# Conditioning sums by transposes and ScalarE, a one-operation GpSimd layer norm and bias-started accumulators in a two-layer hybrid decoder

## The chip, the core and the metric

One NeuronCore of a Trainium2 chip runs the whole program. The metric is the device time of one execution in microseconds, launch to end; the profile's span, from the first instruction to the last, is a little shorter. The engines are named as in the profile: PE (TensorE matmuls) and PEld (its weight loads), DVE (VectorE), ACT (ScalarE), POOL (GpSimd), SP (SyncE, which issues most DMAs).

## What is computed

256 tokens of width 2048 pass through two layers, all in float32. Each layer has a token mixer (forgetting attention in layer 0, sliding-window attention in layer 1) and a gated feed-forward with a short convolution (width 5632). Each of the four sub-layers is modulated by a conditioning vector `c` and closed by a layer norm:

```python
c_act = silu(c)                                   # (1, 2048)
for i in range(2):
    mod = c_act @ ada_w[i] + ada_b[i]             # ada_w[i]: 2048 x 12288
    sh1, sc1, g1, sh2, sc2, g2 = split(mod, 6)
    h = x * (1 + sc1) + sh1
    y = fox_attention(h) if i == 0 else swa_attention(h)
    x = layer_norm(ALPHA * x + (1 + g1) * y, ln_mix_g[i], ln_mix_b[i])
    h = x * (1 + sc2) + sh2
    y = (silu(conv(h @ w_up)[:, :5632]) * conv(h @ w_up)[:, 5632:]) @ w_down
    x = layer_norm(ALPHA * x + (1 + g2) * y, ln_ffn_g[i], ln_ffn_b[i])
```

The twelve vectors of `mod` are called (layer, index) below, index 0 to 5 for sh1, sc1, g1, sh2, sc2, g2. (0, 0) and (0, 1) are made in the opening; the other ten run in the background behind the matmuls of the layers.

## The kernel before

**Weights.** `stream` loads weights as tiles of 256 x 512 (512 KB) on SP's queue into a ring of ten buffers. For each, ACT rounds the tile to `wh` (line 258, the high half), DVE subtracts to get `wl` (line 269, the low half), and PE forms three products per block: high by high, high by low, low by high. With the activations as moving operand (`w_mm`, tile names `ws`) one tile is 24 matmuls of 256 columns; with the weights as moving operand (`x_mm`, `xs`) 12 of 512 columns.

**Order of the work.** `then` and `stream` put closures in the list `work`; `settle` takes them out about two weight tiles behind the loads. Before it runs a closure, `rest` looks through the next ones and writes the `wl` subtractions of up to two coming tiles. `tick` runs after each weight tile and advances the background: `ada_tick` adds `ada["rate"]` to a debt and makes one step of a conditioning vector per whole unit. `pin` keeps an instruction at its place; the others may be moved by the scheduler, which then fixes the order on each engine.

**Conditioning vectors** (`ada_vector`). One vector is 32 steps; each loads 512 KB of `ada_w` (`wa`) and adds its product with `cact` to `acc`, [128, 2048], by one DVE operation (line 384). The 128 partial sums of each column must then be added over partitions. For shifts and scales (columns) PE does it with 16 single-column matmuls against `ones` (`sums`, line 404, which the profile counts as 32 instructions), and DVE adds the bias (`finish`, line 408). (0, 4) and (1, 4) are held: their `sums` run in `release` at the layer norm where they are needed. Gates (rows, index 2 and 5) start from `acc` filled with zeros by POOL (line 373) with the bias loaded into its first row (line 374), and end in four matmuls of `ones` by 512 columns of `acc` (line 394). There is one `acc`.

**Boundaries.** Between two sub-layers PE has nothing to do: `residual` (lines 559 to 566, DVE) multiplies by the gate, adds to `x`, and takes statistics in quarters of 512 columns for the token halves t = 0 and 1; POOL makes the reciprocal deviation `rs` from variance + EPS by a power (lines 568, 569), and for t = 0 the product -mean * rs (571, 572), which ACT needs as bias. `normalise` then works on t = 0 on ACT (line 582) and on t = 1 on DVE (line 584), PE transposes (line 461), and `mod_pair` makes the halves `hH` and `hL` (lines 471 to 476, 84, 85). `between` sets this off; there are three boundaries, called 0 (before the first feed-forward), 1 (before the sliding-window attention) and 2 (before the second feed-forward), and a last layer norm at the end.

## Time and profile before

| What | Value |
|---|---|
| Time, median of 3 runs | 2310.31 us (2304.98 to 2312.66) |
| The profiled execution: its own time / its span | 2308.74 us / 2307.0 us |
| Granted TensorE clock, mean over the span | 0.982 of full speed |
| PE, DVE, ACT, POOL busy | 97%, 78%, 49%, 2% of the span |
| Weight and conditioning tiles read | 728 weight tiles, 320 conditioning tiles of 512 KB |

Stages, by the profile's time: opening and forgetting attention to about 500 us, first feed-forward 510 to 1265, sliding-window attention 1273 to 1544, second feed-forward 1552 to 2290, last layer norm to the end. Times in rows of the profile are in us from the start of the span. A busy PE is not PE at its best: matmuls overlap, and at half clock they are as busy as at full clock, so the column PEclk and the distance from one start to the next are to be read with it.

### The profile page before, as it was taken

How to read it: one execution, taken by the hardware profiler on the slowest of the kernel's cores; microseconds unless marked ns; L12 is line 12 of the kernel's file. 1: busy time of each engine (PE TensorE's matmuls, PEld its weight loads, DVE VectorE, ACT ScalarE, POOL GpSimd, SP SyncE). 2: the span in 40 equal slices, each digit the busy share in tenths (PEclk: the TensorE clock that was granted, in tenths of full speed). 3: DMA queues.
4: the chain of work that ended last, by engine and by line, in shares of the span. 5: the costliest groups of instructions: out<-in, count | busy, mean ns of one | idle time of the engine just before them, and what ended most of it. 6: DMA issues, size and time to landing. Idle time of an engine off the chain costs nothing.

```text
span 2307.0 us, 38669 instructions
## 1 busy us (share of the span) xinstructions
PE 2239.2 (97%) x15061; PEld 2056.8 (89%) x15061; DVE 1803.3 (78%) x2609; ACT 1136.8 (49%) x1685; POOL 43.0 (2%) x79
## 2 busy tenths in 40 slices
PE   6999999999999999999999999999999999999997
PEld 5899988779999988999987778779999988999986
DVE  7788978879977878868889978799887655666656
ACT  1335654445555533445533578845555533455532
POOL 1001000010000000000000000010000000000000
PEclk9899999999999999999999999999999999999999
DMA  9998999968887889878889676678887566666663
GB/s 325 311 332 282 338 329 346 335 217 306 298 280 229 292 318 323 290 239 282 288 276 348 200 237 194 217 265 276 264 277 244 179 193 193 192 187 189 189 194 110
DMA packets 285562, 598.86 MB, mean 260 GB/s; under 512 B 20791, under 2 KB 53817, under 8 KB 285377
## 3 DMA queue, kind: packets, MB, share of 16 engines
q1 hardware_dynamic: 284768, 595.85, 78.3%
q8 instruction: 118, 1.93, 0.3%
q0 software_dynamic: 608, 0.53, 0.1%
q14 instruction: 68, 0.55, 0.1%
HBM read 594.21 MB, written 2.10 MB: 258 GB/s over the span
## 4 chain that ended last, share of the span: by engine, by line
PE 88%; DVE 6%; ACT 2%; issue 1%; DMA 1%; POOL 0%; SPq 0%; DVEq 0%; ACTq 0%; POOLq 0%
PE ws L75 50%; PE xs L75 33%; DVE wl L269 2%; PE sm L75 1%; DVE acc L384 1%; DVE oacc L516 1%; PE cps L75 1%; PE S L75 1%; PE o L75 1%; ACT wh L258 1%; DMA w<-in_fox_w_in_dram 1%; PE sm L461 1%; PE T L655 0%; ACT pr L643 0%; ACT pr L635 0%
## 5 line engine op out<-in xcount | busy, mean ns | idle before, releaser
L269 DVE TENSOR_TENSOR wl<-w,wh 128x1024 fp32r<-128x1024 f32 x728 | 888.4, 1222 | 393.8 <-ACT wh L258 370.0
L258 ACT CAST wh<-w 128x1024 fp32r<-128x1024 f32 x728 | 763.6, 1051 | 859.3 <-PE ws L75 329.9
L75 PE MATMUL ws<-hH,wh 128*128 128x256 f32 x3328 | 941.8, 283 | 6.0 <-ACT wh L258 6.0
L75 PE MATMUL ws<-hL,wh 128*128 128x256 f32 x3328 | 934.8, 281 | 0.0
L75 PE MATMUL ws<-hH,wl 128*128 128x256 f32 x3328 | 932.6, 281 | 2.2 <-DVE wl L269 2.0
L75 PEld LDWEIGHTS ws<-hH,wh 128*128 128x128 f32 x3328 | 632.3, 190 | 10.0 <-ACT wh L258 6.8
L75 PEld LDWEIGHTS ws<-hL,wh 128*128 128x128 f32 x3328 | 632.0, 190 | 2.4 <-issue 1.9
L75 PEld LDWEIGHTS ws<-hH,wl 128*128 128x128 f32 x3328 | 630.4, 190 | 3.5 <-DVE wl L269 3.5
L75 PE MATMUL xs<-wh,gT 128*128 128x512 f32 x1408 | 436.8, 391 | 0.0
L384 DVE SCALAR_TENSOR_TENSOR acc<-wa,cact,acc 128x1024 f32<-128x1024 f32 x308 | 391.0, 1277 | 0.0
L75 PEld LDWEIGHTS xs<-wh,gT 128*128 128x128 f32 x1408 | 265.9, 189 | 55.3
L75 PE MATMUL xs<-wl,gT 128*128 128x512 f32 x704 | 275.1, 391 | 0.0
L75 PEld LDWEIGHTS xs<-wl,gT 128*128 128x128 f32 x704 | 133.0, 189 | 27.5
L75 PE MATMUL xs<-wl,hH 128*128 128x512 f32 x352 | 142.5, 405 | 2.9 <-DVE wl L269 2.9
L75 PE MATMUL xs<-wh,hH 128*128 128x512 f32 x352 | 142.3, 410 | 1.2 <-ACT wh L258 0.9
L75 PE MATMUL xs<-wh,hL 128*128 128x512 f32 x352 | 141.8, 405 | 0.4 <-DVE hL L85 0.4
L75 PE MATMUL xs<-wh,oT 128*128 128x512 f32 x384 | 125.3, 397 | 0.4 <-ACT pT L657 0.3
L985 ACT ACTIVATE u<-ws,ccol 128x256 f32<-128x256 f32 x176 | 96.6, 562 | 57.2 <-PE ws L75 50.2
L986 DVE SCALAR_TENSOR_TENSOR u<-ws,ccol,u 128x255 f32<-128x255 f32 x176 | 82.4, 477 | 19.1 <-ACT u L985 19.1
L75 PEld LDWEIGHTS xs<-wh,oT 128*128 128x128 f32 x384 | 72.8, 190 | 15.7 <-ACT pT L657 0.7
L75 PEld LDWEIGHTS xs<-wl,hH 128*128 128x128 f32 x352 | 67.8, 193 | 19.1 <-DVE wl L269 4.2
L988 DVE SCALAR_TENSOR_TENSOR u<-ws,ccol,u 128x254 f32<-128x254 f32 x176 | 83.2, 477 | 2.0
(211 smaller groups left out, 1568.1 us busy)
## 6 DMA issues: line engine op xcount, KB each, us to landing
w<-in_ffn_w_up_dram SPq DMA_DIRECT2D x352, 512.0 KB, 4.6
wa<-in_ada_w_dram SPq DMA_DIRECT2D x320, 512.0 KB, 5.2
w<-in_ffn_w_down_dram SPq DMA_DIRECT2D x176, 512.0 KB, 5.0
w<-in_fox_w_in_dram SPq DMA_DIRECT2D x96, 512.0 KB, 6.1
wo<-in_ada_w_dram SPq DMA_DIRECT2D x64, 512.0 KB, 7.2
w<-in_swa_w_in_dram SPq DMA_DIRECT2D x40, 512.0 KB, 5.1
w<-in_fox_w_o_dram SPq DMA_DIRECT2D x32, 512.0 KB, 6.4
w<-in_swa_w_o_dram SPq DMA_DIRECT2D x32, 512.0 KB, 5.4
```

What stands on the lines that cost most here:

```text
L75: return nc.tensor.matmul(o, lhsT, rhs, start=start, stop=stop, **kw)
L258: pin(nc.scalar.copy(h, w), False)
L269: pin(nc.vector.tensor_tensor(l, w, f32(h), op=ALU.subtract), False)
L384: pin(nc.vector.scalar_tensor_tensor(ac, wo, cact[:, k:k + 1], ac, op0=ALU.mult, op1=ALU.add), True)
L461: nc.tensor.transpose(o[:, t * P:(t + 1) * P], x[:, t, (k + j) * P:(k + j + 1) * P], ident)
L516: nc.vector.scalar_tensor_tensor(acc[:, v, k % 2, :], w[:, k, :], cact[:, kc:kc + 1], acc[:, v, k % 2, :], op0=ALU.mult, op1=ALU.add)
L985: nc.scalar.activation(u, pf, AF.Identity, bias=cw(CW, f), scale=cw(2, f))
L986: nc.vector.scalar_tensor_tensor(u[:, 1:], pf[:, :S - 1], cw(1, f), u[:, 1:], op0=ALU.mult, op1=ALU.add)
L988: nc.vector.scalar_tensor_tensor(u[:, 2:], pf[:, :S - 2], cw(0, f), u[:, 2:], op0=ALU.mult, op1=ALU.add)
```

## The change

- Four column vectors, (0, 3), (1, 0), (1, 1) and (1, 3), no longer end in `sums`. PE transposes `acc` in 16 blocks of 128 x 128, four into one PSUM bank at a step of the background, and ACT adds each block along its row, with an accumulating activation in place, one step later. The held vectors keep `sums`.
- Gates start from `acc` with the bias broadcast to all 128 partitions by one DMA of 1 MB, instead of the fill and the 8 KB DMA, and two steps of the background pass before the first product. The products use `cactp` = 128 * cact and the closing matmul `onep` = 1/128, so the bias counts once.
- Of the layer norm's scalar work POOL keeps the power alone. DVE adds EPS, and for t = 0 makes -mean * rs, just ahead of the last quarter's statistics of t = 1.
- `rest` counts certain closures as two tiles (`lone`), so the `wl` subtractions of tiles behind a boundary are no longer written ahead of it; the first two behind each boundary keep their place in the program (`behind`).
- The rates of the background are raised in four places: feed-forward 0 from 0.52 to 0.64 and 0.76 to 0.78, the output projection of layer 1 from 0.72 to 0.85.

```diff
+    onep = cst.tile([P, P], F32, name="onep")
+    nc.gpsimd.memset(onep, 1.0 / P)
...
+    cactp = cst.tile([P, KC], F32, name="cactp")
+    nc.gpsimd.tensor_scalar_mul(cactp, cact, float(P))
...
-    def then(fn):
+    def then(fn, alone=False):
+        if alone:
+            lone.add(fn)
...
         for f in items:
+            if f in lone:
+                n = max(n, 2)
             if f in residuals:
...
             def residual_(w=w, h=h, l=l, go=go):
-                pin(nc.vector.tensor_tensor(l, w, f32(h), op=ALU.subtract), False)
+                pin(nc.vector.tensor_tensor(l, w, f32(h), op=ALU.subtract), behind[0] > 0)
+                behind[0] -= 1
...
         if row:
-            pin(nc.gpsimd.memset(acc, 0.0), True)
-            nc.gpsimd.dma_start(acc[0:1, :], a["ada_b"][l:l + 1, v * D:(v + 1) * D])
+            nc.gpsimd.dma_start(acc, a["ada_b"][l, v * D:(v + 1) * D].partition_broadcast(P))
+            yield
+            yield
...
-                mm(ps, ones, acc[:, j * 512:(j + 1) * 512], start=True, stop=True)
+                mm(ps, onep, acc[:, j * 512:(j + 1) * 512], start=True, stop=True)
...
         else:
-            sums()
-            yield
+            tot = sp.tile([P, KC], F32, tag="tot", bufs=1, name="tot")
+            for k in range(0, KC, 4):
+                tb = bank()
+                for j in range(4):
+                    nc.tensor.transpose(tb[:, j * P:(j + 1) * P], part((k + j) * P, P), ident)
+                yield
+                for j in range(4):
+                    o = tb[:, j * P:(j + 1) * P]
+                    nc.scalar.activation(o, o, AF.Identity, accum_out=tot[:, k + j:k + j + 1])
+            yield
+            ps.append(tot)
             finish()
...
             if last:
+                if t == 1 and d == D // 512 - 1:
+                    mu, rs, nm = moments[0]
+                    pin(nc.vector.scalar_tensor_tensor(nm, mu, -1.0, rs, op0=ALU.mult, op1=ALU.mult))
                 nc.vector.bn_stats(stats[:, t, d, :], xs)
...
-                    nc.gpsimd.tensor_scalar_add(rs[:, 0:1], mv[:, 1:2], EPS)
-                    nc.gpsimd.tensor_tensor(rs[:, 0:1], rs[:, 0:1], mhalf, op=ALU.pow)
-                    if t == 0:
-                        nc.gpsimd.tensor_tensor(rs[:, 1:2], rs[:, 0:1], mv[:, 0:1], op=ALU.mult)
-                        nc.gpsimd.tensor_scalar_mul(rs[:, 1:2], rs[:, 1:2], -1.0)
+                    nc.vector.tensor_scalar_add(mv[:, 1:2], mv[:, 1:2], EPS)
+                    nc.gpsimd.tensor_tensor(rs[:, 0:1], mv[:, 1:2], mhalf, op=ALU.pow)
...
-            then(lambda d=d: defer(residual(ps[d], d, gates[l, 2], True)))
-        then(lambda: (flush(), ada.update(gate_free=True)))
+            then(lambda d=d: defer(residual(ps[d], d, gates[l, 2], True)), d == D // WB - 1)
+        then(lambda: (flush(), ada.update(gate_free=True)), True)
...
         modulate(*merged(l, v, g, b, ll), normalise)
+        behind[0] = 2
```

The feed-forward's last residual and flush and the calls of `between` are marked `alone` in the same way.

**PE, vector (1, 1) in the first feed-forward.** Before, the partition sums stand in one piece between the matmuls of the up-projection (`sm` is a PSUM bank, x16 are sixteen calls):

```order
L75 MATMUL ws<-hL,wh 128x256
L75 MATMUL ws<-hH,wl 128x256
L75 MATMUL sm<-ones,acc 128x1 x16
L75 MATMUL ws<-hH,wh 128x256
L75 MATMUL ws<-hL,wh 128x256
```

Now the first of four groups, with the up-projection's matmuls around it:

```order
L75 MATMUL ws<-hH,wh 128x256
L75 MATMUL ws<-hL,wh 128x256
L75 MATMUL ws<-hH,wl 128x256
L433 MATMUL sm<-ident,acc 128x128 x4
L75 MATMUL ws<-hH,wh 128x256
```

The sixteen single-column matmuls of this vector have become four groups of four transposes.

**DVE, boundary 1.** From the last product of the background before the boundary to the first low halves behind it, before (`t`, `stats` and `mv` belong to the residual and its statistics, `wl` to the first tiles of the next stage):

```order
L384 SCALAR_TENSOR_TENSOR acc<-wa,cact,acc 128x1024
L559 TENSOR_TENSOR t<-xs,gate 128x512
L561 TENSOR_TENSOR x<-x,t 128x512
L563 BN_STATS stats<-x 128x6
L559 TENSOR_TENSOR t<-xs,gate 128x512
L566 BN_AGGR mv<-stats 128x2
L269 TENSOR_TENSOR wl<-w,wh 128x1024
L561 TENSOR_TENSOR x<-x,t 128x512
L269 TENSOR_TENSOR wl<-w,wh 128x1024
L563 BN_STATS stats<-x 128x6
L566 BN_AGGR mv<-stats 128x2
L584 TENSOR_SCALAR x<-x,mv,rs 128x512 x3
```

Now the same stretch, first up to the normalisation of t = 1:

```order
L395 SCALAR_TENSOR_TENSOR acc<-wa,cactp,acc 128x1024 x2
L580 TENSOR_TENSOR t<-xs,gate 128x512
L582 TENSOR_TENSOR x<-x,t 128x512
L587 BN_STATS stats<-x 128x6
L590 BN_AGGR mv<-stats 128x2
L592 TENSOR_SCALAR mv<-mv 128x1
L580 TENSOR_TENSOR t<-xs,gate 128x512
L582 TENSOR_TENSOR x<-x,t 128x512
L586 SCALAR_TENSOR_TENSOR rs<-mv,rs 128x1
L587 BN_STATS stats<-x 128x6
L590 BN_AGGR mv<-stats 128x2
L592 TENSOR_SCALAR mv<-mv 128x1
```

and then, directly behind it:

```order
L605 TENSOR_SCALAR x<-x,mv,rs 128x512 x4
L493 TENSOR_SCALAR t<-sm,G,B 128x256 x2
L494 TENSOR_TENSOR hL<-t,hH 128x256 x2
L493 TENSOR_SCALAR t<-sm,G,B 128x256 x2
L494 TENSOR_TENSOR hL<-t,hH 128x256 x2
L277 TENSOR_TENSOR wl<-w,wh 128x1024 x2
```

The two `wl` have moved from the middle of the statistics to behind the first four low halves `hL`, one more product stands ahead of the residual, and all four quarters of t = 1 are normalised in a row instead of three.

**POOL, boundary 0.** Before (`rs` is the reciprocal deviation, `acc` the accumulator of (0, 5)):

```order
L568 TENSOR_SCALAR rs<-mv 128x1
L569 TENSOR_TENSOR rs<-rs,mhalf 128x1
L571 TENSOR_TENSOR rs<-rs,mv 128x1
L572 TENSOR_SCALAR rs<-rs 128x1
L568 TENSOR_SCALAR rs<-mv 128x1
L569 TENSOR_TENSOR rs<-rs,mhalf 128x1
L373 MEMSET acc 128x2048
L374 DMA acc<-in_ada_b_dram 1x16x128
```

Now, with the loads that stand ahead (`rows` are columns of weights for later):

```order
L164 DMA rows<-in_ffn_conv_w_dram 88x128 x3
L165 DMA rows<-in_ffn_conv_b_dram 88x128
L593 TENSOR_TENSOR rs<-mv,mhalf 128x1
L383 DMA acc<-in_ada_b_dram 128x2048
L593 TENSOR_TENSOR rs<-mv,mhalf 128x1
```

The fill is gone, and the DMA into `acc`, which waits for the held sums of (0, 4) on PE, stands ahead of the power of t = 1.

21 lines of the change are left out of this document (11 added, 10 removed).

## The prediction, made before the change was run

> **What bounds the kernel now.** I read the page first, then the busy times and the granted clock by stage, then the chain that ended last, and then the timeline around the two places where PE stands still. The page's busy times and its chain:
>
> ```profile
> PE 2239.2 (97%) x15061; PEld 2056.8 (89%) x15061; DVE 1803.3 (78%) x2609; ACT 1136.8 (49%) x1685; POOL 43.0 (2%) x79
> PE 88%; DVE 6%; ACT 2%; issue 1%; DMA 1%; POOL 0%; SPq 0%; DVEq 0%; ACTq 0%; POOLq 0%
> ```
>
> PE bounds nearly the whole span; what takes work or slow clock from PE in a full stage counts in full, and what speeds up another engine counts only where PE waits. The windows show where that is (busy us of PE, PEld, DVE, ACT and POOL, then the granted clock, the DMA share and GB/s):
>
> ```profile
> 400.00:450.00 50.00, 48.06 (x235) 39.71 (x234) 43.68 (x61) 25.03 (x49) 0.00 (x0) 1.00 0.97 334
> 450.00:500.00 50.00, 45.44 (x188) 35.88 (x187) 39.50 (x42) 16.75 (x16) 0.00 (x0) 0.97 0.86 289
> 500.00:510.00 10.00, 7.19 (x47) 6.25 (x46) 8.99 (x17) 5.78 (x10) 6.53 (x8) 0.71 0.35 114
> 529.60:687.00 157.40, 157.40 (x1348) 157.04 (x1346) 141.59 (x184) 85.47 (x116) 0.00 (x0) 1.00 0.89 301
> 1260.00:1280.00 20.00, 14.66 (x60) 11.31 (x59) 16.40 (x27) 10.03 (x14) 3.61 (x6) 0.83 0.57 214
> ```
>
> The feed-forward (fourth row) has no gap on PE. PE waits at the boundaries (third and fifth row: 2.8 and 5.3 us, and the clock drops too), and somewhat in forgetting attention's output projection (the first two rows), where DMA and DVE are nearly full.
>
> **Part 1, the column sums in the first feed-forward.** The chain shows the sums of (0, 3), (1, 0), (1, 1) and (1, 3) as links of their own (start, us):
>
> ```profile
> 383.00 3.46 PE sm L75 x32
> 855.81 3.48 PE sm L75 x32
> 1013.25 3.88 PE sm L75 x32
> 1186.94 3.52 PE sm L75 x32
> ```
>
> The last three lie in the feed-forward: 3.48 + 3.88 + 3.52 = 10.9 us of PE. What follows them shows in the granted clock; the columns are PE busy, clock, DMA share, GB/s:
>
> ```profile
> 386.30:390.00 3.70, 3.70 (x18) 1.00 0.80 268
> 859.10:862.50 3.40, 3.40 (x10) 0.50 0.38 124
> 1016.10:1022.90 6.80, 6.80 (x34) 0.50 0.53 157
> 1190.20:1193.60 3.40, 3.40 (x10) 0.50 0.59 174
> ```
>
> PE is "busy" through all of them, but behind each of the three the clock stands at half, for 3.4, 6.8 and 3.4 us. Half of that is lost: 1.7 + 3.4 + 1.7 = 6.8 us, of which 0.4 is in the 3.88 already, so 6.4. Behind (0, 3) it stays at 1.00. The cost before is 10.9 + 6.4 = 17.3 us.
>
> The new work is 48 transposes. The nearest row is twelve in one piece at full clock, from this start to the next matmul's:
>
> ```profile
> 1331.45 1.47 PE L934 MATMUL qp<-ident,qq 128*128 128x128 f32 x12
> 1332.68 0.48 PE L75 MATMUL xs<-wh,hL 128*128 128x512 f32 x1
> ```
>
> 1.23 us for twelve is 0.103 each, 4.9 us for 48. PE time alone gives -6.0. Four transposes last 0.41 us, and PE works fully on both sides, so I expect no half clock behind them and count the 6.4 too. I take -12; the bounds are -6.0 (slow windows come anyway) and -12.4. For (0, 3) the same step saves 3.46 - 1.65 = 1.8 us at 383, but behind it, from 430 on, PE waits for DVE and DMA (first two rows of the windows): 0, with -1.8 as a bound.
>
> On ACT the price comes from the attention's exponentials, also 128 x 128 with an accumulator:
>
> ```profile
> L635 ACT ACTIVATE pr<-pr,nm 128x128 f32<-128x128 f32 x96 | 43.4, 453 | 22.4 <-DVE nm L631 22.3
> L635 ACT ACTIVATION_READ_ACCUMULATOR pr<-pr,nm 128x1 f32 x96 | 18.0, 188 | 0.0
> ```
>
> At most 0.64 us each, 64 times, is 41 us in bursts of 2.6. ACT is at 85.47 of 157.40 us in the feed-forward and makes the weight halves two tiles ahead, so one burst a step is covered: 0. If a PSUM bank comes free late, PE waits: up to +3.
>
> **Part 2, the boundaries.** Boundary 1 before, first DVE, then PE:
>
> ```profile
> 1262.42 1.28 DVE L384 SCALAR_TENSOR_TENSOR acc<-wa,cact,acc 128x1024 f32<-128x1024 f32 x1
> 1263.62 0.69 DVE L559 TENSOR_TENSOR t<-xs,gate 128x512 f32<-128x512 f32 x1
> 1266.44 1.16 DVE L269 TENSOR_TENSOR wl<-w,wh 128x1024 fp32r<-128x1024 f32 x1
> 1268.11 1.22 DVE L269 TENSOR_TENSOR wl<-w,wh 128x1024 fp32r<-128x1024 f32 x1
> 1269.25 0.69 DVE L563 BATCH_NORM_STATS2 stats<-x 128x6 f32<-128x512 f32 x1
> 1269.96 0.26 DVE L566 BATCH_NORM_AGGREGATE mv<-stats 128x2 f32<-128x24 f32 x1
> 1271.21 1.46 DVE L584 TENSOR_SCALAR x<-x,mv,rs 128x512 f32<-128x512 f32 x3 [0.98 <-POOL rs L569]
> 1273.15 1.00 DVE L472 TENSOR_SCALAR t<-sm,G,B 128x256 f32<-128x256 f32 x2 [0.48 <-ACT hH L471]
> 1276.31 0.54 DVE L476 TENSOR_SCALAR t<-sm,G,B 128x256 f32<-128x256 f32 x1
> ```
>
> ```profile
> 1270.61 2.33 PE L461 MATMUL sm<-ident,x 128*128 128x128 f32 x8 [5.01 <-ACT x L582]
> 1273.76 0.63 PE L75 MATMUL xs<-wl,hH 128*128 128x512 f32 x1
> 1276.07 0.39 PE L75 MATMUL xs<-wh,hH 128*128 128x512 f32 x1
> ```
>
> The two `wl` leave the statistics, but they are 1.2 us each and one more product of 1.2 (1262.42 to 1263.62) now comes ahead, so the residual begins at 1264.8. Each half's steps take 0.7 each (statistics to aggregate, 1269.25 to 1269.96): t, x, statistics, then aggregate and EPS in an estimated 0.5, 2.65 in all; twice that ends at 1270.1. The power on POOL, 0.58 (first row of the fence on boundary 0), puts the normalisation at 1270.7, only 0.5 earlier than 1271.21. The new product -mean * rs on DVE waits for POOL's power of t = 0, with the last statistics queued behind it; the power can start at 1267.5 and needs 0.58, the product comes at 1268.9, so it adds nothing. What is late next is `wl`: PE's second matmul of the new stage needs it. Before it had long been made, at 1269.3; now it stands behind four normalisations (to 1272.6), two pairs of steps from L472 to the next L476 (1273.15 to 1276.31, 3.16) and its own 1.2, so at 1277.0. PE starts its second matmul there, not at 1273.76. Before it lost some time on `hL` and was at its sixth, at 1276.07; now it gets there at 1278.4 at full clock, or 1279.8 at half. I take +3.5. Bounds: -0.5 (`wl` is not waited for), +5.4 (a further 3.4 us at half clock).
>
> Boundaries 0 and 2 have a stall of another kind; POOL, DVE and PE at boundary 0:
>
> ```profile
> 505.12 0.58 POOL L569 TENSOR_TENSOR rs<-rs,mhalf 128x1 f32<-128x1 f32 x1
> 505.64 1.80 POOL L373 MEMSET acc<- 128x2048 f32 x1
> 507.74 0.62 POOL L374 DMA_DIRECT2D acc<-in_ada_b_dram  x1 [0.29 <-POOL acc L373]
> ```
>
> ```profile
> 505.73 2.00 DVE L584 TENSOR_SCALAR x<-x,mv,rs 128x512 f32<-128x512 f32 x1 [0.69 <-POOL rs L569]
> ```
>
> ```profile
> 500.24 3.63 PE L75 MATMUL sm<-ones,acc 128*128 128x1 f32 x32
> 511.22 0.28 PE L75 MATMUL ws<-hH,wl 128*128 128x256 f32 x1
> ```
>
> The first normalisation takes 2.00 us while POOL fills `acc`; three take 1.46 at boundary 1. Without the fill this 1.5 us goes. The DMA into `acc` now stands ahead of the power of t = 1 and waits for the held sums (500.24 + 3.63 = 503.9); 0.62 for its issue and 0.58 for the power put the normalisation at 505.1, its end at 505.7 instead of 507.7. But again `wl` is next: 505.1 + 1.9 (1271.21 to 1273.15) + 3.16 + 1.2 = 511.4, against 511.22 for PE's first matmul with `wl` before. The 2 us are given back. PE stands between and may keep half clock longer, so I take +1 for each of the two; bounds -2 (`wl` is not waited for) and +2.
>
> **Part 3, the rest.** In the first half of feed-forward 0, 1344 matmuls of weight tiles at 24 are 56 tiles in 157.4 us, 2.81 each, with 141.59 / 56 = 2.53 of DVE. A rate 0.12 higher adds 0.12 x 1.28 = 0.15: 2.68 of 2.81. It fits, with little room: +0.5, bounds 0 and +4. For the broadcast of 1 MB the nearest rows are:
>
> ```profile
> ln<-in_ln_ffn_g_dram SPq DMA_DIRECT2D x4, 512.0 KB, 4.5
> acc<-in_ada_b_dram POOLq DMA_DIRECT2D x4, 8.0 KB, 2.5
> ```
>
> Half of its size lands in 4.5 us; two steps of the background, over 4 us at 2.81 a tile, pass before the first product. At 334 GB/s 1 MB costs 3.1 us of the queues, which matters only for (0, 2) at 178 us, when they are full: +0.5, bounds 0 and +3. In the opening POOL's `onep` and `cactp` stand ahead of fills that DVE needs, but DVE waits longer for its first weights:
>
> ```profile
> 9.68 0.35 DVE L514 TENSOR_SCALAR oacc<-wo,cact 128x256 f32<-128x256 f32 x1 [6.15 <-DMA wo<-in_ada_w_dram]
> ```
>
> Those 6.15 us cover two small operations: 0, and without that cover about 1. The last layer norm loses POOL steps and gains DVE steps of like size: 0, within 0.5.
>
> Sum: -12 + 3.5 + 2 + 0.5 + 0.5 = -5.5. The profiled execution took 2308.74 us (span 2307.0), so 2303.2 of its kind. The median is 1.6 above it: 2304.8.
>
> **The rivals.** *The boundaries keep their gain*: -12 - 0.5 - 4 + 1 = -15.5, 2294.8. The normalised x is earlier at all three; against it stands the order on DVE. Chance 0.20. *Half clock behind each restart*: PE, idle until `wl`, keeps 0.50 for one or two more stretches of 3.4 us at three places, 5 to 10 us more: 2310 to 2315, 2312 in the middle. For it: 6.8 us at half clock at 1016. Chance 0.17. *DVE becomes the bound* in feed-forward 0, if its unevenness eats the 5% left: 157 x 0.05 = 8 in place of the 0.5, 2312.3; against it, PE has no gap at 90%. Chance 0.05.
>
> *The transposes slow the clock too*, the case on the slower side: each of the twelve groups in the feed-forward is followed by 3.4 us at half clock, 1.7 lost, 20.4 in all: -5.5 + 20.4 = +15, 2325. It decides from about four such groups. Against it: the twelve transposes at 1331.45 run at full pace to the next matmul. Chance 0.06. The Trainium skill, "TensorE: Matmul & The Clock Gate", Part 4: PE-mode transpose, says that full clock does not engage for transposes, as they do not count as PE work. By that rule a longer run of them would cost what the single-column matmuls cost; no run here yet shows four among full matmuls in the feed-forward.
>
> **How the numbers follow.** The forecast has 0.52, with its own range of -10 to 0 (2300 to 2310). A difference of 0.3%, 6.9 us, is about what a measurement can tell. Of the forecast a little over a third lies beyond it, 0.20; with the first rival 0.40 faster. Slower are the transposes' case and part of the half clock's: 0.10. The rest, 0.50, is within 0.3%. The range runs from the first rival's 2294 to 2315, the end of the half-clock case.
>
> **What would show it.** Right: no half clock around 855, 1013 and 1187 us in the granted clock, groups of four transposes near 0.41 us apart from their neighbours; at boundaries the normalisation earlier by 0.5 and 2 us, and PE's first wait behind it ended by `wl`. Wrong: half clock behind the groups, PE waiting for a PSUM bank that ACT holds, or PE's first `wl` matmul earlier than before against its transposes.

## The result, and the profile after

The changed kernel takes 2284.04 us (median of 6 runs, 2281.01 to 2287.92), the kernel before 2311.21 in the same comparison (6 runs, 2304.47 to 2312.66): a ratio of 0.9891 (95% interval 0.9874 to 0.9908), 25 us less. The prediction was 2304.8 with a range of 2294 to 2315, so the time lies 10 us below the range. The profiled execution took 2283.99 us, its span is 2282.1, its mean granted clock 0.988 against 0.982 before.

The page's busy times after, then the windows that answer to those of before (PE, PEld, DVE, ACT, POOL busy, granted clock, DMA share, GB/s):

```profile
PE 2222.3 (97%) x14997; PEld 2043.3 (90%) x14997; DVE 1801.9 (79%) x2621; ACT 1156.2 (51%) x1813; POOL 25.4 (1%) x61
```

```profile
400.00:450.00 50.00, 50.00 (x246) 41.89 (x246) 46.04 (x65) 25.51 (x50) 0.00 (x0) 1.00 0.94 340
450.00:500.00 50.00, 44.47 (x199) 36.54 (x197) 41.57 (x57) 20.21 (x24) 1.74 (x3) 0.89 0.79 284
490.00:500.00 10.00, 8.81 (x52) 8.01 (x50) 7.08 (x20) 6.52 (x11) 1.74 (x3) 0.62 0.26 105
520.00:677.40 157.40, 157.21 (x1323) 154.87 (x1322) 142.76 (x185) 84.81 (x118) 0.00 (x0) 1.00 0.89 305
1240.00:1260.00 20.00, 16.39 (x76) 13.07 (x75) 17.61 (x32) 12.27 (x19) 1.11 (x2) 0.91 0.48 168
```

PE is still the bound at 97%, with 17 us less of work. The feed-forward (fourth row) is full at a granted clock of 1.00, and DVE, 142.76 instead of 141.59 us there, still fits. Boundary 1 (last row) has 3.6 us without PE instead of 5.3 and a clock of 0.91 instead of 0.83. Boundary 0 (third row) has gained nothing in clock: 0.62, where the prediction's row of before has 0.71.

**The sums.** PE at the first group of vector (1, 0), and the windows behind this group and the last of (1, 3):

```profile
814.29 0.39 PE L75 MATMUL xs<-wh,gT 128*128 128x512 f32 x1
814.52 0.60 PE L433 MATMUL sm<-ident,acc 128*128 128x128 f32 x4
814.88 0.48 PE L75 MATMUL xs<-wh,gT 128*128 128x512 f32 x1
```

```profile
814.90:818.30 3.40, 3.40 (x18) 2.81 (x16) 1.23 (x1) 2.63 (x10) 0.00 (x0) 1.00 0.59 175
...
1138.70:1142.10 3.40, 3.40 (x18) 2.81 (x17) 3.20 (x8) 3.06 (x12) 0.59 (x1) 1.00 0.78 263
```

Four transposes take 0.36 us from their start to the next matmul's (0.41 was forecast), and the clock behind them is 1.00. ScalarE's part is 64 times 262 + 194 ns, 0.46 us each instead of at most 0.64:

```profile
L437 ACT ACTIVATE sm<-sm x64: 251/262/272, 381.8 to 1141.1; 128x128 f32<-128x128 f32 x64
L437 ACT ACTIVATION_READ_ACCUMULATOR sm<-sm x64: 180/194/197, 382.0 to 1141.3; 128x1 f32 x64
```

**Boundary 1**, DVE and then PE:

```profile
1242.40 0.69 DVE L580 TENSOR_TENSOR t<-xs,gate 128x512 f32<-128x512 f32 x1 [0.74 <-PE xs L75]
...
1248.41 1.92 DVE L605 TENSOR_SCALAR x<-x,mv,rs 128x512 f32<-128x512 f32 x4 [0.66 <-POOL rs L593]
...
1253.39 2.36 DVE L277 TENSOR_TENSOR wl<-w,wh 128x1024 fp32r<-128x1024 f32 x2
```

```profile
1247.51 0.66 PE L482 MATMUL sm<-ident,x 128*128 128x128 f32 x4 [2.43 <-ACT x L603]
1249.02 0.66 PE L482 MATMUL sm<-ident,x 128*128 128x128 f32 x4 [0.85 <-DVE x L605]
1250.00 0.68 PE L75 MATMUL xs<-wh,hH 128*128 128x512 f32 x1 [0.33 <-ACT hH L492]
1250.48 0.63 PE L75 MATMUL xs<-wl,hH 128*128 128x512 f32 x1
```

From the last quarters of the residual to the normalisation of t = 1 it is 6.0 us (1242.40 to 1248.41) instead of 7.6 (1263.62 to 1271.21). And PE's second matmul, the first on a low half, runs at 1250.48, while the two `wl` behind the boundary are made from 1253.39 on. They are not the ones it needs. PE's first wait at this boundary is ended by ScalarE's normalisation of t = 0: 2.43 us instead of the 5.01 in the prediction's row at 1270.61.

**Boundary 0**, POOL:

```profile
490.06 0.57 POOL L593 TENSOR_TENSOR rs<-mv,mhalf 128x1 f32<-128x1 f32 x1 [284.35 <-DVE mv L592]
494.83 0.61 POOL L383 DMA_DIRECT2D acc<-in_ada_b_dram  x1 [4.19 <-PE sm L75]
495.45 0.57 POOL L593 TENSOR_TENSOR rs<-mv,mhalf 128x1 f32<-128x1 f32 x1
```

This came as forecast: the DMA waits for the held sums and the power of t = 1 stands behind it. The clock did not. The stretch at half clock around this boundary, before and then after:

```profile
504.20:510.90 6.70, 4.22 (x17) 3.42 (x18) 5.76 (x14) 4.98 (x9) 3.18 (x4) 0.50 0.26 83
```

```profile
492.40:502.60 10.20, 9.01 (x41) 8.21 (x41) 7.49 (x20) 5.20 (x10) 1.18 (x2) 0.50 0.26 104
```

It is three times 3.4 us long instead of twice, and the extra 3.4 us cost up to half of that, 1.7.

### The profile page after: what moved, and what is told of

The parts are those of the page before. It is cut to its first block, busy times and chain, and to the rows that moved or that the text cites. A ratio compares the mean times of both kernels' runs of the same rounds, so it can differ in the third digit from the quotient of the medians.

```text
span 2282.1 us, 38648 instructions
## 1 busy us (share of the span) xinstructions
PE 2222.3 (97%) x14997; PEld 2043.3 (90%) x14997; DVE 1801.9 (79%) x2621; ACT 1156.2 (51%) x1813; POOL 25.4 (1%) x61
## 5 line engine op out<-in xcount | busy, mean ns | idle before, releaser
L395 DVE SCALAR_TENSOR_TENSOR acc<-wa,cact,acc 128x1024 f32<-128x1024 f32 x180 | 228.7, 1279 | 0.0
L395 DVE SCALAR_TENSOR_TENSOR acc<-wa,cactp,acc 128x1024 f32<-128x1024 f32 x128 | 163.0, 1279 | 1.8 <-DMA acc<-in_ada_b_dram 1.8
```

Of the source, the lines that this page charges most:

```text
L395: pin(nc.vector.scalar_tensor_tensor(ac, wo, (cactp if row else cact)[:, k:k + 1], ac, op0=ALU.mult, op1=ALU.add), True)
```

## Where the time went, by stage

To compare stages, the table takes the start of the same weight matmul, counted from the program's first (numbers 1000, 2300, 2600, 7540, 8000, 8380, 8600 and 13,700), and subtracts its start in the profiled execution of before; each cell is what a stage adds, in us. Eight kernels of the experiments below are in it too; for the others the text gives single stages, worked out in the same way. "Sliding, 1" has boundary 1 and the first half of the sliding-window stage.

| Kernel | opening | layer 0 from 240 us, with output projection | boundary 0 | feed-forward 0 | sliding, 1 | sliding, 2 | boundary 2 | feed-forward 1 |
|---|---|---|---|---|---|---|---|---|
| changed | -4.9 | -5.3 | +0.9 | -11.1 | -6.0 | -0.2 | +0.1 | +2.1 |
| before + sums | -2.6 | -5.4 | +1.2 | -11.5 | -4.1 | +5.5 | +17.5 | +5.9 |
| before + sums + rates | -4.6 | -5.4 | +1.6 | -10.5 | -2.6 | +2.8 | +0.3 | +2.0 |
| before + rates | -2.8 | +3.1 | +0.9 | +2.5 | -3.1 | +2.9 | +0.3 | 0.0 |
| before + order | +0.3 | -0.1 | -0.7 | +3.3 | -2.5 | +0.1 | -0.9 | +0.2 |
| changed, old order | -2.7 | -5.1 | +1.2 | -10.4 | -3.6 | -0.2 | -1.3 | +0.1 |
| changed, no turns | +1.2 | -5.5 | +0.8 | -9.1 | -4.1 | +2.9 | +0.3 | +0.2 |
| changed, split sums | -5.0 | -2.4 | -0.7 | -5.7 | -6.4 | -0.2 | -1.4 | +0.1 |
| changed, bias on SP | -3.0 | -5.2 | -1.3 | -11.1 | -6.9 | -0.2 | -2.0 | 0.0 |

The opening's column can't be put down to the change. Windows of 30 to 130 us of before, of before + order and of before + sums + rates, in which every engine has the same instructions in the same order far beyond this stretch, and of the changed kernel:

```profile
30.00:130.00 100.00, 91.02 (x561) 84.82 (x561) 78.31 (x170) 30.77 (x37) 0.00 (x0) 0.85 1.01 330
```

```profile
30.00:130.00 100.00, 89.41 (x557) 83.35 (x557) 77.69 (x169) 30.76 (x37) 0.00 (x0) 0.86 0.99 327
```

```profile
30.00:130.00 100.00, 89.21 (x593) 83.07 (x594) 80.98 (x176) 32.48 (x40) 0.00 (x0) 0.91 1.03 341
```

```profile
30.00:130.00 100.00, 89.22 (x594) 82.85 (x594) 81.28 (x177) 32.80 (x40) 0.00 (x0) 0.91 1.03 343
```

The first three have clocks of 0.85, 0.86 and 0.91 with the same instructions, and lie 4.9 us apart by 130 us. The last kernel's -4.9 is no different: the variant further down with the low half of tile 0 behind the boundary has the changed kernel's opening, instruction for instruction, and +0.9 there. Differences in the opening are left out of what follows; so are those in the second feed-forward (2 us in two kernels, 5.9 in before + sums), whose cause is open. Half clock comes in stretches of 3.4 us, each worth 1.7 us, and their number differs too: at boundary 0 it is three in the changed kernel and in before + sums, and two in before and with the split sums, though before + sums has the boundary of before and the split sums that of the changed kernel. So a difference of up to 2 us in one cell can be the execution's own.

## The experiments

Ratios are to runs of the kernel before on the same chip, with a 95% interval; a small difference is read from the stage, since the total has an uncertainty of some 4 us. The stages are those of one profiled execution, which can lie off its kernel's median: 6.3 us below it for the split sums, 5.4 above for before + order, 4.8 above for before + sums.

**The sums alone**: the new branch of `ada_vector` put into before, with nothing else of the change.

```diff
-            sums()
-            yield
+            tot = sp.tile([P, KC], F32, tag="tot", bufs=1, name="tot")
...
+            ps.append(tot)
             finish()
```

> The kernel before with the new sums alone (four column vectors by transposes and ScalarE), everything else as before. If the sums are worth what the prediction gave them, the three groups in the first feed-forward go with their half-clock stretches: 11.5 us less there (3.3, 4.9 and 3.4 at 856, 1013 and 1187 us), opening and boundaries as before, 2311.2 -> about 2299.7. Rival, the sums also move the background: the added steps of (0, 3) shift (0, 4) into another place and the output projection of forgetting attention loses its waits too, about 5 us more, 2295. Rival, the half clock would have come anyway: only PE time, 6 us, 2305, with half-clock stretches of 3.4 us still in the feed-forward.

Measured: 2310.37 us, 1.0007 (0.9998 to 1.0016). The feed-forward gains its 11.5 us and the output projection 5.4, and all of it is gone by the end. DVE and PE of this kernel at boundary 2:

```profile
1531.07 10.78 DVE L384 SCALAR_TENSOR_TENSOR acc<-wa,cact,acc 128x1024 f32<-128x1024 f32 x9
```

```profile
1540.71 3.57 PE L75 MATMUL sm<-ones,acc 128*128 128x1 f32 x16 [13.45 <-DVE acc L384]
```

A vector now takes five turns for its sums instead of one. At the old rates (1, 4) is still nine products short when the last statistics of boundary 2 are done, and they are made there in a row, with PE idle for 13.45 us and the clock at 0.50 from 1529.3 to 1556.5. The expectation saw the two gains and not this price.

**Sums and rates**, both put into before.

```diff
-            then(lambda i=i: ada.update(rate=((1.4,1.4,1.8,1.8), (0.72,)*4)[l][i]))
+            then(lambda i=i: ada.update(rate=((1.4,1.4,1.8,1.8), (0.85,)*4)[l][i]))
...
-            then(lambda: ada.update(rate=(0.52, 0.4)[l]))
+            then(lambda: ada.update(rate=(0.64, 0.4)[l]))
...
-                ada["rate"] = (0.76, 0.4)[l]
+                ada["rate"] = (0.78, 0.4)[l]
```

> The kernel before with the new sums and the new rates, without the gates, the layer norm's operations and the order. Theory: with the sums alone, the gain of 18 us up to boundary 2 is given back there, because vector (1, 4), whose turns come later by the steps that the sums now take, is not ready and PE waits 13.5 us for its products; the rates are there for this. So here the 11.5 us of the feed-forward and about 5 of the output projection of forgetting attention stay: 2308 - 17 = about 2291. Rival, the rates cost as much as they give (DVE fuller in the feed-forward and in the output projection of layer 1): 2300 or more.

2292.26 us, 0.9932 (0.992 to 0.9945). Boundary 2 costs 0.3 instead of 17.5. The first theory holds.

**The rates alone.**

> The kernel before with the new rates alone. The prediction on record gave them 0.5 us of cost, 0 to 4. If they are of use only because the new sums take more steps, nothing is gained here: 2308 to 2312. Rival, they gain by themselves, as vectors come off the end of the sliding-window stage where DVE is full: 2300 to 2306.

2310.66 us, 1.0003 (0.9992 to 1.0015): worth nothing by themselves.

**The changed kernel with the old rates.**

> The changed kernel with the old rates. Theory: as with the sums alone, (1, 4) is not ready at boundary 2; the two steps that a gate now waits make it later still by a step or two of 1.2 us: 13 to 20 us of PE standing there, 2284 -> 2297 to 2305. Rival, the order or the layer norm frees enough steps: under 3 us, 2284 to 2287. A third, by the prediction on record where the higher rates cost 0.5 us: 2283.5.

2306.95 us, 1.000 (0.999 to 1.001): by the medians 23 us of the gain are gone, by the ratio all of it, more than expected; boundary 2 alone is 19.7 us worse than in the changed kernel.

**The changed kernel with the old sums.**

> The changed kernel with the old sums (16 single-column matmuls in one piece). If the sums are worth 11.5 us whatever stands around them, 2284.0 -> 2295.5, with half clock for 3.4 to 6.8 us behind each of (1, 0), (1, 1) and (1, 3) and nothing else moved. Rival, the parts help each other: the rates were raised for vectors that take more steps, so with the old sums vectors end earlier than needed and move other waits, a difference of 5 us or more from 11.5, to be seen in the output projection (430 to 470 us) or in the sliding-window stage.

2306.37 us, 0.9999 (0.9989 to 1.0009): 22 us by the medians and the whole gain by the ratio, not 11.5. The feed-forward loses 9.9, the output projection 7.7, the second half of the sliding-window stage 3.0. So the rival holds: the value of the sums is not that of one stage.

**Splitting or transposing?** The changed kernel with single-column matmuls, in four groups:

```diff
-                for j in range(4):
-                    nc.tensor.transpose(tb[:, j * P:(j + 1) * P], part((k + j) * P, P), ident)
+                for j in range(k, k + 4):
+                    pin(mm(ps[0][:, j:j + 1], part(j * P, P), ones[:, 0:1], start=True, stop=True))
                 yield
...
```

> The changed kernel with the sums of the four vectors by single-column matmuls again, but in four groups of four at the same steps as the transposes, without ScalarE. It tells the splitting from the operation. If a stretch of 3.5 us of single-column matmuls is what halves the clock, groups of 0.87 us do not, and only PE time comes back: 3 x (3.5 - 1.7) = 5 us in the feed-forward, about 2290. If single-column matmuls of any length halve it, twelve groups give up to 12 x 1.7 = 20 us on top, 2305 to 2310. If the transposes are not faster than the matmuls, no difference.

2292.91 us, 0.9938 (0.9924 to 0.9951). PE at the first group of (1, 0), and the windows behind it and behind the last group of (1, 3):

```profile
816.24 0.95 PE L75 MATMUL sm<-ones,acc 128*128 128x1 f32 x8
```

```profile
816.90:820.30 3.40, 3.40 (x17) 2.85 (x17) 1.23 (x1) 0.79 (x2) 0.00 (x0) 1.00 0.52 141
1145.40:1148.80 3.40, 3.40 (x17) 2.81 (x17) 3.28 (x8) 1.42 (x4) 0.59 (x1) 1.00 0.82 300
```

The clock stays at 1.00 behind all twelve groups of 0.81 us in the feed-forward. There this kernel gains 5.7 of the 11.1 us: half of the stage's gain is the splitting, and the other half, 5.4 us, is the shorter work of the transposes (twelve times 0.81 - 0.36 us), as expected. That holds for the profiled execution, which was the fastest of five (2286.63 us); by the ratio this kernel is 11 us slower than the changed one, and where the others lose the rest is not shown.

**Long runs of transposes**: each made eight times, 32 in a piece.

```diff
-                for j in range(4):
-                    nc.tensor.transpose(tb[:, j * P:(j + 1) * P], part((k + j) * P, P), ident)
+                for j in range(32):
+                    nc.tensor.transpose(tb[:, j % 4 * P:(j % 4 + 1) * P], part((k + j % 4) * P, P), ident)
```

> The changed kernel with each transpose of the four vectors made eight times, so that a group is 32 transposes in one piece, 3.3 to 3.9 us, as long as the 16 single-column matmuls before. Work alone: 28 more transposes of 0.103 us, 2.9 us in each of twelve groups in the feed-forward and four outside, 35 to 46 us: 2319 to 2330, at full clock. If transposes do not count as work for the clock (the rule that the Trainium skill, TensorE: Matmul & The Clock Gate, Part 4, states), each group is followed by 3.4 us at half clock, 1.7 lost and its own transposes slower towards its end: 20 us or more on top, 2340 to 2360.

2332.95 us, 1.0108 (1.0094 to 1.0122). One group on PE, and the windows behind it and behind two groups of (0, 3) that follow each other (6.9 us of transposes):

```profile
827.58 3.65 PE L433 MATMUL sm<-ident,acc 128*128 128x128 f32 x32
```

```profile
399.60:403.00 3.40, 3.40 (x20) 2.81 (x19) 0.00 (x0) 2.39 (x10) 0.00 (x0) 1.00 0.00 0
831.10:833.80 2.70, 2.70 (x14) 2.18 (x13) 0.00 (x0) 1.47 (x8) 0.00 (x0) 1.00 0.61 195
```

3.41 us of transposes leave the clock at 1.00, where 3.48 us of single-column matmuls in the kernel before were followed by 0.50. The added work is 28 x 0.107 x 16 = 48 us, and 48.9 were measured. The Trainium skill, "TensorE: Matmul & The Clock Gate", Part 4: PE-mode transpose, says that full clock does not engage for transposes, as they do not count as PE work in the same way. In these runs the clock stays at 1.00 (the profile lists them as MATMUL on `ident`, and shows nothing of a mode).

**The order alone**, put into before: `lone`, `behind` and the marks.

```diff
+            if f in lone:
+                n = max(n, 2)
...
+        behind[0] = 2
```

> The kernel before with the new order alone (closures that count as two tiles, the first two low halves behind a boundary pinned). The prediction on record says that PE then waits for the low half of its first tile at each boundary: 1 to 3.5 us later each, 2314 to 2318. Rival, formed from the trace after: the low half of tile 0 is still made ahead of the boundary and only tile 1 stands behind it, so PE does not wait: boundary 1 earlier by 1 to 3 us, boundaries 0 and 2 by 0 to 1, 2306 to 2310, and the sliding-window stage behind boundary 1 loses its stall at 1333 to 1340 only if that stall comes from this order (then 6 us less, about 2302).

2303.46 us, 0.9985 (0.9974 to 0.9996): 3.5 us less by the ratio, whose interval just leaves out 1, where the prediction had it slower. The first half of the sliding-window stage, with boundary 1, is 2.5 us shorter. PE's first wait at the boundary is 2.73 us instead of 5.01, and GpSimd's four operations for t = 0 take 2.0 us in all instead of 3.1; before, a `wl` on DVE ran beside the first of them, which took 1.06 us and takes 0.22 here.

**The changed kernel with the old order.**

> The changed kernel without the new order. If the order only helps boundary 1 and the rest is due to others, about 1 to 4 us slower than the changed kernel, 2285 to 2288. If the order also took away the stall in the sliding-window stage, 6 us more, 2292. By the prediction on record, where the order costs 3.5 us at boundary 1 and 2 us at each of the others, it would be faster, 2277 to 2282.

2286.02 us, 0.9906 (0.9893 to 0.9919). The stage at boundary 1 gives back 2.4 us. The stall in the sliding-window stage does not return, so it does not come from the order.

**The low half of tile 0 behind the boundary too**: what the prediction believed the program to be.

```diff
             if f in lone:
-                n = max(n, 2)
+                n = max(n, 3)
```

> The changed kernel with closures marked alone counting as three tiles, so that the low half of tile 0 too stands behind each boundary. This makes the program what the prediction took it to be. By its working PE then waits for the low half: at boundary 1 about 3.5 us, at the others 2 us each, with the first matmul on a low half 2 us or more behind the first transposes' matmuls: 2284 -> 2289 to 2293, more with half clock. Rival, DVE is early enough anyway (the normalisation is what PE waits for, and ScalarE's high halves): under 2 us, 2283 to 2286.

2285.72 us, 0.990 (0.9884 to 0.9916). By stage boundary 0 is 0.3 us later than in the changed kernel, the stage of boundary 1 0.1 earlier, boundary 2 0.8 earlier. Boundary 1 here, DVE and PE:

```profile
1260.16 3.49 DVE L277 TENSOR_TENSOR wl<-w,wh 128x1024 fp32r<-128x1024 f32 x3
```

```profile
1256.87 1.22 PE L75 MATMUL xs<-wh,hH 128*128 128x512 f32 x2
1257.88 3.03 PE L482 MATMUL sm<-ident,x 128*128 128x128 f32 x18
1261.12 0.44 PE L482 MATMUL sm<-ident,x 128*128 128x128 f32 x2 [0.20 <-ACT t L496]
1261.43 0.50 PE L75 MATMUL xs<-wl,hH 128*128 128x512 f32 x1
```

The `wl` of tile 0 is ready at 1261.4, and the first matmul on it starts then. But PE is idle for only 0.20 us: the transposes of later blocks, which it owes anyway, have been put ahead. The wait that the prediction priced at 3.5 us costs nothing even where it exists.

**The layer norm's scalar work on GpSimd again**, in the changed kernel.

```diff
-                    nc.vector.tensor_scalar_add(mv[:, 1:2], mv[:, 1:2], EPS)
-                    nc.gpsimd.tensor_tensor(rs[:, 0:1], mv[:, 1:2], mhalf, op=ALU.pow)
+                    nc.gpsimd.tensor_scalar_add(rs[:, 0:1], mv[:, 1:2], EPS)
+                    nc.gpsimd.tensor_tensor(rs[:, 0:1], rs[:, 0:1], mhalf, op=ALU.pow)
...
```

> The changed kernel with the layer norm's scalar work on GpSimd as before (EPS, power, product and sign there). At boundary 1 two more GpSimd operations of 0.55 and up to 1.15 us stand between the last statistics and the normalisation, and the power of t = 1 is queued behind them: 1 to 2 us at each of three boundaries, 2 to 6 us in all, 2286 to 2290. By the prediction on record, where statistics and not GpSimd set the end: 0 to 1.5 us, 2284 to 2285.5.

2286.41 us, 0.9896 (0.988 to 0.9912), not to be told from the changed kernel by the total; by stage it is 0.8 us longer at boundary 1 and 0.2 at boundary 0, and 1.1 shorter at boundary 2.

**The gates as before**, in the changed kernel: fill, 8 KB bias, no turns.

```diff
-            nc.gpsimd.dma_start(acc, a["ada_b"][l, v * D:(v + 1) * D].partition_broadcast(P))
-            yield
-            yield
+            pin(nc.gpsimd.memset(acc, 0.0), True)
+            nc.gpsimd.dma_start(acc[0:1, :], a["ada_b"][l:l + 1, v * D:(v + 1) * D])
...
```

> The changed kernel with the gates' accumulators filled and the bias in one row, as before. The fill stretches a normalisation at boundaries 0 and 2 from 0.55 to 2.0 us and, in GpSimd's order, may stand ahead of the power of t = 1: 1.5 to 4 us at each, 2287 to 2292. By the prediction on record the gain of the missing fill is given back at once and the broadcast of 1 MB costs 0.5 us: 2283 to 2284. The first quarter of the opening is the same program in both but for the two constants, so a difference there is not the change's.

2290.44 us, 0.9919 (0.9902 to 0.9935). The loss is not where it was expected. The fill stretches a normalisation at boundary 0 to 2.02 us again, but the boundary is 1.8 us shorter than in the changed kernel, with two stretches of half clock instead of three; the first feed-forward loses 2.7 us and the second half of the sliding-window stage 3.0.

**Only the two turns left out**; the broadcast stays.

```diff
             nc.gpsimd.dma_start(acc, a["ada_b"][l, v * D:(v + 1) * D].partition_broadcast(P))
-            yield
-            yield
```

> The changed kernel without the two turns that a gate waits after its DMA. Each gate's products come two steps earlier, and DVE waits for the DMA (5 to 8 us from issue to landing): up to 4 us at (0, 5) and (1, 2), less where PE has tiles in hand. The turns also place the background against the attention: the runs with the gates as before, which lack them, show a stall of 2.1 us for ScalarE's pT and a half-clock stretch at about 1415 us that the changed kernel does not have. If the turns decide that, it comes back here: 2287 to 2291. If it is the fill and the filled accumulator: 2284 to 2286.

2291.57 us, 0.9922 (0.9906 to 0.9939): the same loss as with the gates as before, and in the same two stages (2.0 and 3.1 us), so it is the turns, not the fill. The waits of PE between 540 and 600 us (us in total, times, longest), which the changed kernel does not have; then PE at 1418 us and the window behind it:

```profile
PE ws L75 <- DVE wl L277: 1.9, 2, 1.6
```

```profile
1418.84 0.66 PE L953 MATMUL qp<-ident,qq 128*128 128x128 f32 x4 [1.94 <-ACT pT L676]
```

```profile
1419.80:1423.20 3.40, 3.40 (x10) 2.67 (x9) 2.80 (x5) 1.47 (x5) 0.00 (x0) 0.53 0.57 186
```

and the same place of the changed kernel:

```profile
1407.71 0.66 PE L955 MATMUL qp<-ident,qq 128*128 128x128 f32 x4 [0.75 <-ACT pT L678]
```

Without the turns the products of (0, 5) reach DVE while it still catches up behind boundary 0, and PE waits 1.9 us for low halves. In the sliding-window stage one attention head's chain comes 1.2 us later against PE, the wait grows from 0.75 to 1.94, and half clock follows for 3.4 us (0.53). Why ScalarE is that much later there was not taken apart; the runs show that it goes with the place of the background's turns (it is there in before + rates, before + sums + rates, without the turns, and with the gates as before, but also in the changed kernel with the old sums, which has the turns).

**What still limits boundaries 0 and 2.** Five variants of the changed kernel: the held vectors summed early, first without, then with a pause of the background until the boundary; the bias on SP's queue (`nc.sync.dma_start` for `nc.gpsimd.dma_start`); and two mixtures. First without the pause, by leaving `HELD` empty:

> The changed kernel with (0, 4) and (1, 4) no longer held: they are summed by transposes and ScalarE as soon as their last product is made, 4 and 8 tiles ahead of their boundary. In the changed kernel the sums of the held vectors run at boundaries 0 and 2 (3.9 us of PE at 489.7, the last third at half clock), GpSimd's DMA into the accumulator waits for them, and the power of t = 1 behind it starts 2.7 us late. If that is what sets the restart, both boundaries gain 2 to 4 us and one half-clock stretch each of 1.7: 2284 -> 2277 to 2280. Rival, the added steps and the earlier start of the next gate fill DVE in the output projections: same or slower, 2284 to 2290.

2300.35 us, 0.9962 (0.9949 to 0.9975): slower than the changed kernel. DVE at boundary 0 stands for the next gate's DMA, its products are queued ahead of the residual, and PE waits:

```profile
487.18 2.48 DVE L395 SCALAR_TENSOR_TENSOR acc<-wa,cactp,acc 128x1024 f32<-128x1024 f32 x2 [4.44 <-DMA acc<-in_ada_b_dram]
```

```profile
507.35 2.19 PE L482 MATMUL sm<-ident,x 128*128 128x128 f32 x8 [8.74 <-ACT x L603]
```

Holding a vector also keeps the background out of the boundary. With the pause (`ada["held"]` set once such a vector is summed):

> The changed kernel with the held vectors (0, 4) and (1, 4) summed by transposes and ScalarE as soon as they are complete, while the background still pauses until the boundary, as in the changed kernel. In the run without the hold, DVE stood 4.4 us for the gate's DMA and the gate's products were queued ahead of the residual at boundary 0; with the pause neither happens. If the sums at the boundary are what delays the power of t = 1 (by 2.7 us) and brings two more half-clock stretches (3.4 us lost) at each of boundaries 0 and 2: 2 to 5 us at each, 2284 -> 2275 to 2280. If the restart is set by other work anyway: 2283 to 2285.

2281.59 us, 0.989 (0.9872 to 0.9907). Boundary 0 is 3.9 us shorter and boundary 2 2.4, but the output projection loses 2.2 and the sliding-window stage's second half 2.0, and the total is that of the changed kernel. The bias on SP's queue:

> The changed kernel with the gate's 1 MB bias broadcast issued on SP's queue instead of GpSimd's, nothing else. It takes the DMA that waits for the held sums from ahead of the power of t = 1. If that queue is what delays the normalisation of t = 1, it starts 2.2 to 2.7 us earlier at boundaries 0 and 2, of which PE can use what is left once its own held sums are done, 0.5 to 2 us at each: 2280 to 2283. If SP, waiting for the sums, holds back weight loads: slower by up to 4 us, 2288.

2279.93 us, 0.9877 (0.9856 to 0.9897). POOL at boundary 0:

```profile
492.20 0.57 POOL L593 TENSOR_TENSOR rs<-mv,mhalf 128x1 f32<-128x1 f32 x1 [284.51 <-DVE mv L592]
494.99 0.55 POOL L593 TENSOR_TENSOR rs<-mv,mhalf 128x1 f32<-128x1 f32 x1 [2.22 <-DVE mv L592]
```

The power of t = 1 now starts 2.8 us after that of t = 0, not 5.4. Both boundaries are shorter by about 2 us, and no other stage is longer but the opening. Of these 2 us, 1.7 at each go with one stretch of half clock less; at boundary 0:

```profile
494.80:501.50 6.70, 6.45 (x30) 5.88 (x30) 5.05 (x16) 4.95 (x9) 0.55 (x1) 0.50 0.59 228
```

The split sums, which keep the bias on GpSimd's queue, also have two stretches at both places, with -0.7 and -1.4 against -1.3 and -2.0 here. So the earlier power is shown, but of the time that the queue is worth only about 0.6 us at each is left once the clock is set aside, and the totals do not tell the two kernels apart. Both steps together, and then both at boundary 2 only:

> Both steps together on the changed kernel: the held vectors summed early with the background pausing, and the bias broadcast on SP's queue. If both worked on the same wait (the power of t = 1 behind the held sums), together they give no more than one of them: 2279 to 2282. If the early sums give the clock and SP's queue the wait, they add: 2275 to 2278.

2283.18 us, 0.9896 (0.9881 to 0.9912): they do not add. Boundaries 0 and 2 together gain 6.0 us over the changed kernel, but the output projection and the sliding-window stage lose 4.2, as with the pause alone.

> The changed kernel with the bias broadcast on SP's queue, (1, 4) summed early with a pause, (0, 4) held as in the changed kernel. At boundary 0 the early sums cost 2 us in the output projection before they gave 4, at boundary 2 they gave 2.6 against 1.0 for SP's queue alone: 1 to 2 us below the run with SP's queue alone, 2278 to 2279. If the transposes of (1, 4) in the sliding-window stage bring a stall of ScalarE there (2 us between 1380 and 1500 in the run with the pause), 2280 to 2282.

2278.71 us, 0.9881 (0.9867 to 0.9896). It and the one with only the bias on SP's queue are the two fastest; their intervals overlap with each other and with the changed kernel's, and what speaks for the simpler one is that it loses nothing in the output projection and the sliding-window stage.

## Why the prediction was wrong, point by point

**The sums in the first feed-forward, -12: right.** -11.1 for the stage, with the rates' cost in it. The clock stays full behind the transposes, as forecast; the case in which they slow it was tested with eight times the length and did not come. The price on ScalarE, 0, holds.

**(0, 3) at 383 us, 0: wrong; -5.3.** The step that failed is that PE's waits behind it, from 430 us on, take back the 1.8 us of shorter work. They are not taken back, and 3.5 more come. PE's waits for low halves between 430 and 475 us (us in total, times, longest), first before and then after, change:

```profile
PE xs L75 <- DVE wl L269: 6.1, 4, 2.3
```

```profile
PE xs L75 <- DVE wl L277: 4.3, 2, 3.5
```

That explains 1.8 us, and 0.4 more were a wait for `hL` before. The sums alone bring the whole -5.4 (before + sums). That (0, 4) comes later by the new sums' turns may be why the waits are shorter, but it is not shown: the split sums take the same turns and PE still waits 6.0 us there; their -2.4 goes with the missing of a stretch of half clock (466.6 to 470.0 us in the kernel before). The remaining 1 us was not traced. Nor was the clock behind (0, 3) safe: the granted clock at this place in before + rates, with the same instructions up to there as before, is

```profile
382.40:389.20 6.80, 6.80 (x23) 5.85 (x23) 3.83 (x5) 0.00 (x0) 0.00 (x0) 0.51 0.70 239
```

The 1.00 in the prediction was one execution's; half clock at the same place costs 3.4 us in this execution of before + rates.

**Boundary 1, "`wl` is next", +3.5: wrong in sign; about -2.5.** Three steps failed. The order shown ahead of the prediction has two `wl` behind the normalisation, and I took the first for tile 0's. It is a later tile's: a marked closure counts as two, so one more low half is still written ahead of the boundary, and PE's `xs<-wl,hH` at 1250.48 runs three microseconds before that `wl`. Had it been tile 0's, the price would still have been nothing (1257.88 in the run made for it): PE has the transposes of later blocks to do. And the product that comes ahead of the residual does not delay it, since the residual waits 0.74 us for PE there. What remains is the statistics without low halves between them, which the prediction had as a bound of -0.5 through the normalisation of t = 1. PE's first wait hangs on t = 0, a path that the sum does not follow, and that wait fell from 5.01 to 2.43 us.

**Boundaries 0 and 2, +1 each: near in size, by luck.** +0.9 and +0.1. The power of t = 1 does wait for the held sums and starts at 495.45, as forecast. The step that failed is "again `wl` is next": at boundary 0 PE runs its first matmul on a low half at 500.30 without a wait for it. These are the held sums and that matmul in the changed kernel:

```profile
489.95 4.58 PE L75 MATMUL sm<-ones,acc 128*128 128x1 f32 x32
...
500.30 0.42 PE L75 MATMUL ws<-hH,wl 128*128 128x256 f32 x1
```

From the start of the one to the other it is 10.35 us instead of 10.98 (500.24 to 511.22). That small gain was given back by the clock: the last 2 us of the held sums run at 0.50, and half clock lasts to 502.6, one stretch longer than before. How many stretches come is in part the execution's own, as the table's kernels show, so +0.9 is no measure of the forecast.

**The sliding-window stage: not in the sum; about -3.5 of the -6.0.** The kernel before had two waits there, followed by half clock at 1337, which the prediction did not look for:

```profile
1334.54 0.73 PE L75 MATMUL xs<-wh,hH 128*128 128x512 f32 x2 [0.93 <-ACT wh L258]
1336.38 0.50 PE L75 MATMUL xs<-wl,hH 128*128 128x512 f32 x1 [1.11 <-DVE wl L269]
```

They are gone in the kernels of the table whose background stands elsewhere. With new sums and rates alone a wait with half clock comes back at 1414 (+2.8); in the changed kernel, with the two turns of the gates, it is not there.

**The rates, +0.5, and the gates' turns, +0.5: wrong in kind.** Each was priced as added work. The rates alone neither cost nor gain, but they are what lets the sums keep their gain: without them 23 of the 25 us are lost by the medians and all by the ratio, 19.7 of them at boundary 2. The prediction counted ScalarE's and PE's time for the new sums and not the four turns more that a vector takes, which move its due time. The turns of the gates, taken as a cost hidden by other work, are worth 7 us by the totals (0.9922 against 0.9891, intervals just overlapping) and 5 by two stages.

By stage the sum that I gave as -5.5 is -19.5 without the opening. The part of the difference that the boundaries' sign made is 6, the output projection 5, the sliding-window stage 3.5. The totals differ by 25 us. The other 5 stand in the opening of the two profiled executions; that they belong to the change is not shown. The kernel before may also lose more at (0, 3) and in its sums in executions other than the profiled one. Of the rivals, the nearest time was that of the boundaries that keep their gain (2294.8), but of the -4.5 that it had for the boundaries only about -1.5 came; the rest came from places that no case named.

## What to carry to other kernels

Where background work is handed out in turns, an edit that changes the number of turns moves everything behind it and its due times: count the turns up to each point where the result is needed, and judge the edit only together with the rates. Cut a run of small matmuls into pieces before looking for a faster operation; here that was 5.7 of the 11.1 us of the feed-forward. And before a `wl` or any other operand is called late, find out which tile it belongs to, and what else the waiting engine still has to do.

## What the runs showed of the hardware that was not expected

- Of the 16 runs of 3.5 us or more of single-column matmuls that make the sums of the four vectors in before, before + order, before + rates and the changed kernel with the old sums, 13 go with one or two stretches of 3.4 us at half clock, which begin towards their end or within 2 us behind them. Groups of 0.81 us with full matmuls between them do not (1.00, one execution), and neither do 3.41 or 6.9 us of 128 x 128 transposes (1.00).
- A wait of PE of 0.75 us left the clock at 1.00, one of 1.94 us at a like place was followed by 0.53 for 3.4 us. So a delay of 1.2 us on another engine can cost 2.9. The length alone does not decide: in the kernel before a wait of 2.27 us that ended at 461.1 left the clock at 1.00, and one of 1.79 us that ended at 465.95 was followed by 0.50 from 466.6 to 470.0.
- The same instructions in the same order got a granted clock of 0.85, 0.86 or 0.91 between 30 and 130 us, and 1.00 or 0.51 behind the sums at 383 us, in different executions. A cause read from one profiled execution can be that execution's own.
